# Where the output projection's operand splits stand in the queues, and which engine does the last group's late gating

## The chip, the cores and the metric

The kernel runs on one core of one Trainium2 chip. The metric is the device time of one launch in microseconds (us). A core has engines that work side by side, each through its own queue in order: PE (TensorE, matrix products), ACT (ScalarE), DVE (VectorE), POOL (GpSimd) and SP, which here issues nearly all DMA transfers. An engine whose next instruction waits on a semaphore lets everything behind it in its queue wait too.

## The reference

One decoder layer in float32 over 2048 tokens (16 learned meta tokens go ahead of them), width 1024:

```python
hn = rms_norm(h, norm_g)
proj = einsum('bld,de->ble', hn, w_in)                # 1024 -> 4096
cx, cb, cc, cg, q, k, v, rg = split(proj, 8)          # 512 columns each
conv_out = cb * short_conv(cc * cx, conv_w) * silu(cg)
ret_out  = head_group_norm(retention(rot(q), rot(k), v), ret_norm_g) * silu(rg)
mixed = concatenate([conv_out, ret_out], -1)
h = h + einsum('ble,ed->bld', mixed, w_out)           # 1024 -> 1024
out = rms_norm(h, final_g)[:, N_META:]
```

What matters here is the last product, `mixed` times `w_out`, and the gating `conv_out = (...) * silu(cg)` of the last convolution group, which feeds it.

## The kernel before, in words

**Products.** Each float32 operand is split into a high part (an ACT cast) and a low part (a DVE subtraction), both by `split` (lines 117 to 126), and a product is three matmuls: low by high, high by low, high by high. Blocks of 2 by 2 are multiplied with seven instead of eight block products, so both operands need sums and differences of their blocks. A block product is 12 matmuls of 128x128 by 128x512 (`product` in `quad`, line 275, and in `quads`, line 323).

**Weights and moving operands.** In the output stage the rows of `mixed` are the stationary side ("weights": tiles `wh`, `wl`, in rings of `RING = 3` buffers each, filled by `weight_parts`), and `w_out` is the moving side (tiles `mh`, `ml`, one buffer for each of the seven operands, "slots"). A weight buffer comes free when the product three before it is done.

**Two row halves, then the output.** The loop over `r` runs eight units (heads and convolution groups) for each half of the rows. The last convolution group of a half is called with `last=True`: its products are taken, but its gating is left for later: a function is put in the list `kept`. Then comes the output for eight pairs of row blocks (a pair is 256 rows). Pairs 0 and 1 are done together, turn by turn, by `quads` (turn i does product i of pair 0, then product i of pair 1); pairs 2 to 7 follow one by one in `output`, each with one `quad`.

**The opening of the output.** `moving_in_turn` loads and splits the first block of `w_out` (slot 0), splits the first weights of both pairs ("leading"), then slot 1, and returns steps that are run inside `quads`. `open_output` is run behind turn 0 and traces the splits of three prepared operands: `sums(m, 1)` into slot 2 (tiles `t`), `sums(m, 0)` into slot 3 and `sums(m, 2)` into slot 4 (tiles `held`, loaded long before). Slot i is first used in turn i.

**The late gating.** For each of the last group's two column blocks j: the gate is multiplied by the row factors `rr`, ACT takes Silu of it, the convolution result is multiplied by `rr`, the two are multiplied ("join", on POOL in any case), and the result is stored to `mixed`. In row half 1 the function is called behind pair 2 with POOL for all multiplications. Block j = 0 is in rows that pairs 4 and 5 read, j = 1 in rows that pairs 6 and 7 read. Row half 0's gating is called in `close_sums`, with DVE.

**An output pair.** `stationary` makes four sums of the pair's blocks on POOL (`sa`, `ra`), `rows` adds the products to the residual: for products that need two terms, POOL adds the copied term `tc` to `yo` (line 1129), DVE adds the PSUM bank (line 1135). Product 4 and product 6 of a pair accumulate in the same bank, so product 6 can't start until DVE has added the bank as product 4 left it. Then come squares on ACT, the row factor `rf` on POOL (line 420) and the final scaling on ACT (line 1170) and DVE (line 1177).

**What sets the order.** The order of each queue is written at build time by a planner: it takes instructions in the order in which the code traces them, as they become ready by its own costs, with the timeline simulation that the last lines of `kernel` ask for. `tc.issue_after(ins)` puts everything that a block traces on the engine of `ins` behind `ins` in that engine's queue, and nothing else; instructions on other engines, DMA issues on SP among them, are not held by it. `queued` does so for several instructions. The names that carry instructions for this: `lowered[0]` (the last DVE split), `copied[0]` (the last ACT copy of a bank), `summed[0]` (the last POOL sum of a pair's blocks), `leads[0]` (pair 0's split of this turn), `loaded[0]` and `line[0]` (DMA issues).

Of the kernel before, what the change touches and what calls it, by code (L numbers as in the profile page):

```python
# [12 lines left out]
AF = mybir.ActivationFunctionType  # L13
# [66 lines left out]
def hybrid_trunk(ctx: ExitStack, tc: tile.TileContext, t, out: bass.AP, chunk_decay):  # L80
# [5 lines left out]
    nc = tc.nc  # L86
# [18 lines left out]
    def brief(name="b"):  # L105
        return sb.tile([P, HB + 128], F32, name=name, tag="b", bufs=BRIEF)[:, :HB]

    lowered, third, fifth, given, summed = [None], [None], [None], [None, None], [None]

    @contextmanager  # L110
    def queued(instructions):
        with ExitStack() as order:
            for ins in instructions:
                order.enter_context(tc.issue_after(ins.ins))
            yield

    def split(hi, lo, src, scale=None, eng=nc.vector):

        if scale is None:
            nc.scalar.copy(out=hi, in_=src)  # L120
            lowered[0] = eng.tensor_tensor(out=lo, in0=src, in1=hi.bitcast(F32), op=ALU.subtract)  # L121
            return
        scaled[0] = nc.scalar.mul(hi, src, scale)
        nc.vector.scalar_tensor_tensor(
            out=lo, in0=src, scalar=scale, in1=hi.bitcast(F32), op0=ALU.mult, op1=ALU.subtract
        )
# [71 lines left out]
    def moving_in_turn(load, scale, sums, ws):  # L198


        m = [[] for _ in range(8)]

        def blocks(half, j, kts=range(KH)):
            for kt in kts:
                k = half * KH + kt
                parts(m, BLOCK[half][j], kt, load(k, j), scale(k) if scale else None)

        blocks(0, 0)
        leading = [next(a) for a in ws]
        blocks(1, 0, range(KH // 2))  # L210
        with tc.issue_after(copied[0].ins):
            blocks(1, 0, range(KH // 2, KH))
        steps = [
            lambda: sums(m, 1), lambda: sums(m, 0), lambda: sums(m, 2), lambda: blocks(1, 1), lambda: sums(m, 3),
        ]
        return m, leading, steps
# [93 lines left out]
    def quads(ws, w, m, takes, between=()):  # L310


        between = iter(between)
        banks = [[None, None] for _ in ws]
        copies = [None for _ in ws]

        def product(n, i, bank, first):
            wh, wl = w[n]
            for kt in range(KH):
                ks = slice(kt * P, (kt + 1) * P)  # L320
                mh, ml = m[i][kt]
                for s, (a, b) in enumerate(((wl, mh), (wh, ml), (wh, mh))):
                    nc.tensor.matmul(  # L323
                        bank, a[:, ks], b, start=first and kt == 0 and s == 0, stop=kt == KH - 1 and s == 2,
                        skip_group_check=not first,
                    )

        def copy(bank):
            c = sb.tile([P, HB], F32, name="tc", tag="tc", bufs=COPIES)
            copied[0] = nc.scalar.copy(out=c, in_=bank)  # L330
            return c

        for i in range(7):
            for n in range(len(ws)):
                if i < 2:
                    banks[n][i] = ps_proj()
                product(n, i, banks[n][i in (1, 3, 5)], i in (0, 1, 3))
            w = [next(a, None) for a in ws[:1]]
            leads[0] = lowered[0]
            w += [next(a, None) for a in ws[1:]]  # L340
            for n, take in enumerate(takes):
                bank = banks[n][i in (1, 3, 5)]
                if i == 0:
                    copies[n] = copy(bank)
                elif i == 1:
                    take(0, 0, bank, copies[n])
                elif i == 2:
                    copies[n] = [copy(bank)]
                elif i == 3:
                    copies[n].append(copy(bank))  # L350
                elif i == 4:
                    take(1, 1, bank, copies[n][1])
                elif i == 5:
                    take(0, 1, bank, copies[n][0])
                else:
                    take(1, 0, bank, None)
            next(between, idle)()
# [285 lines left out]
    def store_mixed(r, j, kt, m):  # L643
        d = mixed[2 * r + j]
        nc.sync.dma_start(
            d[:, :, kt // KH, :, kt % KH, :].rearrange("a i p c -> p a i c"),
            m.rearrange("p (a i c) -> p a i c", a=2, i=2),
        )
# [77 lines left out]
    kept = []  # L726

    def conv_group(g, r, m, f, blocks, ahead, steps=(), last=False):


        def go_on():
            next(factors_ahead[0], None)

        def behind(quad, *own):
            return [lambda n=n: (own[n](), go_on() if (quad, n) in steps else None) for n in range(3)]

        u = [gen("u") for _ in range(2)]
        rr, rr2 = ([a[:, j * HB : (j + 1) * HB] for j in range(2)] for a in f[:2])
        held = [None]
        behind_head = r == 0 and len(waiting[1]) + len(waiting[0]) > 0  # L740

        def mul(eng, out, a, b):
            eng.tensor_tensor(out=out, in0=a, in1=b, op=ALU.mult)  # L743

        def take(i, j, pp, c):
            s = u[j][:, 2:]
            if c is None:
                mul(nc.vector, s, pp, s)
            elif i == 1:
                add(nc.vector, c, pp, c)  # L750
                held[0] = c
            else:
                add(nc.vector, s, pp, c)
                with queued((fifth[0],) if behind_head and j == 0 else ()):
                    mul(nc.vector, s, s, rr2[j])
                if j == 1:
                    mul(nc.gpsimd, s, s, held[0])

        blocks, meta = blocks
        quad(stationary(blocks, keep=kept_sums(2 * (NG + g), r)), m, take, behind(0, lambda: finish_late(behind_head and not waiting[0]), idle, idle))  # L760
        catch_up(0)
        if meta:
            meta_carry(g, meta)
        carry(u, g, r)
        cs = [taps(u[j], g) for j in range(2)]
        gates = []

        ungated = []

        def gated():  # L770
            if last:
                return
            j, c = gates.pop()
            nc.scalar.activation(c, c, AF.Silu)
            mul(nc.gpsimd, cs[j], cs[j], rr[j])
            mul(nc.gpsimd, cs[j], cs[j], c)

        def take(i, j, pp, c):
            if i == 0:
                if last:  # L780
                    gate = brief("cg")
                    add(nc.vector, gate, pp, c)
                    ungated.append(gate)
                    return
                add(nc.vector, c, pp, c)
                mul(nc.vector, c, c, rr[j])
                gates.append((j, c))
                if j == 1:
                    gated()
                return  # L790
            if c is not None:
                add(nc.vector, c, pp, c)
                pp = c
            taken[0] = nc.vector.tensor_tensor(out=cs[j], in0=pp, in1=cs[j], op=ALU.mult)

        n = 2 * (NG + g) + 1
        quad(stationary(load_raw(w_loads(n, r)), keep=kept_sums(n, r)), m, take, behind(1, idle, gated, idle))
        blocks = ahead()
        def store():
            for j in range(2):  # L800
                store_mixed(r, j, g, cs[j])

        def gate_late(eng):
            for j, gate in enumerate(ungated):
                mul(eng, gate, gate, rr[j])
                nc.scalar.activation(gate, gate, AF.Silu)
                mul(eng, cs[j], cs[j], rr[j])
                mul(nc.gpsimd, cs[j], cs[j], gate)
            return store

        if last:
            kept.append(gate_late)
        else:
            store()
        return blocks
# [416 lines left out]
    for r in range(NR):  # L1232
# [82 lines left out]
        else:  # L1315
# [10 lines left out]

            def close_sums(t4=first[4]):
                t4()
                with tc.issue_after(lowered[0].ins):
                    store_kept = kept.pop()(nc.vector)  # L1330
                with tc.issue_after(loaded[0].ins):
                    store_kept()

            first = [(ws, leading), open_sums, first[3], close_sums]
            between = (), idle, idle, idle
# [44 lines left out]
                a[0](i, j, in_line)  # L1380

    def open_output():
        for a in first[:3]:
            a()
        fetch((0, 0))

    def fourth():
# [11 lines left out]
    quads(ws, leading, m, [a[1] for a in two], (open_output, idle, fourth, fifth_pair))  # L1399
    for a in two:  # L1400
        a[3]()
    for pair in range(2, SEQ // (2 * P)):
        output(pair, m, final_g)
        if pair == 2:
            with tc.issue_after(summed[0].ins):
                kept.pop()(nc.gpsimd)()


# [36 lines left out]
```

## Time and profile before

| | |
|---|---|
| median of 3 runs | 864.91 us (864.87 to 866.22) |
| profiled execution | 866.39 us, of which span 864.60 us |
| instructions | 12843 |
| PE busy | 850.8 us (98%) |
| DVE busy | 688.9 us (80%) |
| ACT busy | 498.7 us (58%) |
| POOL busy | 286.7 us (33%) |
| mean granted PE clock | 0.994 |

The span is what lies between the first and the last instruction; the execution's own time has some more around it. A row of the timeline gives the start and the duration in us, engine, line, operation, output<-inputs, and in brackets the idle time before it with what ended it. Matmul rows overlap: each is shown with about 0.39 us, while they start every 0.227 us at full clock. A row of the stretches gives for each engine the busy time and the number of instructions, then the granted PE clock as a share of full speed. Output pair 0 and 1 lie between 698.9 and 738.7 us, pair 2 begins at 738.7 us.

### The profile page before, as it was taken

The numbers are of one execution on the slowest core, as the hardware profiler recorded it, in microseconds if no ns is written. First come the engines' busy times: TensorE is split into PE (matmuls) and PEld (weight loads), VectorE is DVE, ScalarE is ACT, GpSimd is POOL, SyncE is SP. The second block draws the span as 40 slices with busy tenths as digits, with TensorE's granted clock in tenths as the row PEclk, the third lists the DMA queues.
The fourth block names the chain that finished last, engine by engine and source line by source line (L and its number), as shares of the span: only waits on it lengthen the run. The fifth ranks groups of instructions, "written<-read, shape, count | busy, mean of one in ns | idle before, by whom it ended". The sixth has DMA issues, their size and how long they took to land.

```text
span 864.6 us, 12843 instructions
## 1 busy us (share of the span) xinstructions
PE 850.8 (98%) x4192; PEld 703.0 (81%) x4192; DVE 688.9 (80%) x1209; ACT 498.7 (58%) x903; POOL 286.7 (33%) x230
## 2 busy tenths in 40 slices
PE   9999999999999999999999999999999989999996
PEld 6778888878887878888888888888888878778885
DVE  6798989889887977999688788877665777876774
ACT  7875648474845655965673848444333656545453
POOL 0022332323245554000001003240523013987873
PEclk9999999999999999999999999999999999999999
DMA  9736357565777743966565756558646666356432
GB/s 323 243 124 170 94 145 217 145 185 183 183 242 233 254 148 110 364 220 159 116 166 161 207 148 167 171 147 287 181 140 183 240 207 223 124 193 191 151 130 78
DMA packets 143779, 158.88 MB, mean 184 GB/s; under 512 B 60192, under 2 KB 78176, under 8 KB 143712
## 3 DMA queue, kind: packets, MB, share of 16 engines
q1 hardware_dynamic: 143136, 157.67, 59.7%
q8 instruction: 33, 0.54, 0.3%
q10 hardware_dynamic: 576, 0.40, 0.1%
q14 instruction: 34, 0.28, 0.1%
HBM read 103.50 MB, written 41.94 MB: 168 GB/s over the span
## 4 chain that ended last, share of the span: by engine, by line
PE 95%; DVE 1%; issue 1%; POOL 1%; ACT 0%; DMA 0%; ACTq 0%; POOLq 0%; DVEq 0%
PE pj L275 72%; PE pj L323 9%; PE pj L405 5%; PE ms L1030 2%; PE ms L1019 2%; PE ms L1029 2%; PE ms L1006 2%; PE ms L579 1%; DVE ml L121 1%; DMA ra<-in_w_in 0%; DVE wl L121 0%; POOL cg L743 0%; PE ms L453 0%; POOL yo L129 0%; PE ms L609 0%
## 5 line engine op out<-in xcount | busy, mean ns | idle before, releaser
L275 PE MATMUL pj<-mh,wl 128*128 128x512 f32 x952 | 374.2, 393 | 2.4 <-DVE wl L121 2.4
L275 PE MATMUL pj<-mh,wh 128*128 128x512 f32 x952 | 372.1, 391 | 0.0
L275 PE MATMUL pj<-ml,wh 128*128 128x512 f32 x952 | 371.5, 390 | 0.0
L120 ACT CAST wh<-ra 128x512 fp32r<-128x512 f32 x244 | 151.1, 620 | 247.9 <-PE pj L275 175.0
L121 DVE TENSOR_TENSOR wl<-ra,wh 128x512 fp32r<-128x512 f32 x244 | 206.9, 850 | 59.9 <-ACT wh L120 58.7
L275 PEld LDWEIGHTS pj<-mh,wl 128*128 128x128 f32 x952 | 179.2, 188 | 40.5 <-DVE wl L121 2.9
L275 PEld LDWEIGHTS pj<-mh,wh 128*128 128x128 f32 x952 | 179.1, 188 | 37.2
L275 PEld LDWEIGHTS pj<-ml,wh 128*128 128x128 f32 x952 | 179.2, 188 | 36.4
L132 POOL TENSOR_TENSOR ra<-ra 128x512 f32<-128x512 f32 x42 | 64.9, 1544 | 78.1 <-PE ms L579 38.6
L1042 POOL TENSOR_TENSOR rp<-rs,neg_half 128x4 f32<-128x4 f32 x16 | 18.4, 1150 | 140.2 <-DVE rs L129 140.1
L282 ACT COPY tc<-pj 128x512 f32<-128x512 f32 x102 | 59.1, 580 | 0.1
L129 POOL TENSOR_TENSOR sa<-ra 128x512 f32<-128x512 f32 x21 | 31.0, 1477 | 55.7 <-DMA ra<-in_w_in 36.3
L323 PE MATMUL pj<-mh,wl 128*128 128x512 f32 x112 | 44.5, 397 | 2.6 <-DVE wl L121 2.6
L323 PE MATMUL pj<-mh,wh 128*128 128x512 f32 x112 | 44.2, 395 | 0.0
L323 PE MATMUL pj<-ml,wh 128*128 128x512 f32 x112 | 44.1, 394 | 0.0
L1146 POOL TENSOR_TENSOR z<-yo,final_g 128x512 f32<-128x512 f32 x16 | 26.3, 1646 | 51.2 <-DVE yo L1135 49.7
L132 POOL TENSOR_TENSOR ra<-sa,ra 128x512 f32<-128x512 f32 x21 | 30.0, 1430 | 31.2 <-DVE wl L121 23.0
L1135 DVE TENSOR_TENSOR yo<-pj,yo 128x512 f32<-128x512 f32 (+1 forms) x33 | 22.1, 672 | 17.4 <-POOL yo L129 8.4
L1046 DVE TENSOR_SCALAR pm<-ms,mv,rp 128x128 f32<-128x128 f32 x64 | 21.9, 405 | 9.1 <-POOL rp L1042 9.1
L1177 DVE SCALAR_TENSOR_TENSOR yo<-yo,rf,final_g 128x512 f32<-128x512 f32 (+1 forms) x17 | 20.1, 1193 | 10.2 <-POOL rf L420 9.4
L323 PEld LDWEIGHTS pj<-mh,wl 128*128 128x128 f32 x112 | 21.4, 191 | 7.6 <-DVE wl L121 3.2
L129 POOL TENSOR_TENSOR yo<-yo,tc 128x512 f32<-128x512 f32 x18 | 26.4, 1474 | 2.7 <-ACT tc L282 2.4
(171 smaller groups left out, 1235.4 us busy)
## 6 DMA issues: line engine op xcount, KB each, us to landing
ra<-in_w_in SPq DMA_DIRECT2D x110, 256.0 KB, 3.0
ra<-sums_a SPq DMA_DIRECT2D x56, 256.0 KB, 3.1
x<-in_xT SPq DMA_DIRECT2D x44, 256.0 KB, 4.9
sums_a<-ra SPq DMA_DIRECT2D x42, 256.0 KB, 2.1
yo<-in_x SPq DMA_DIRECT2D x32, 256.0 KB, 4.7
ra<-mixed SPq DMA_DIRECT2D x30, 256.0 KB, 3.0
w<-in_w_out SPq DMA_DIRECT2D x28, 256.0 KB, 4.7
ra<-in_x SPq DMA_DIRECT2D x16, 256.0 KB, 3.4
```

The costliest lines, as they stand in the source:

```text
L120: nc.scalar.copy(out=hi, in_=src)
L121: lowered[0] = eng.tensor_tensor(out=lo, in0=src, in1=hi.bitcast(F32), op=ALU.subtract)
L129: eng.tensor_tensor(out=out, in0=a, in1=b, op=ALU.add)
L132: return eng.tensor_tensor(out=out, in0=a, in1=b, op=ALU.subtract)
L275: nc.tensor.matmul(bank, a[:, ks], b, start=first and kt == 0 and n == 0, stop=kt == KH - 1 and n == 2, skip_group_check=not first,)
L282: copied[0] = nc.scalar.copy(out=c, in_=bank)
L323: nc.tensor.matmul(bank, a[:, ks], b, start=first and kt == 0 and s == 0, stop=kt == KH - 1 and s == 2, skip_group_check=not first,)
L405: nc.tensor.matmul(banks[n][i], a[:, ks], b, start=half + kt + s == 0, stop=half == 1 and kt == KH - 1 and s == 2,)
L1046: nc.vector.tensor_scalar(out=y[:, cs], in0=o[:, cs], scalar1=mv[:, c, 0:1], scalar2=rp[:, c, :], op0=ALU.subtract, op1=ALU.mult,)
L1135: last[0] = nc.vector.tensor_tensor(out=y[:, cs], in0=pp[:, cs], in1=y[:, cs], op=ALU.add)
L1146: nc.gpsimd.tensor_tensor(out=ys[i][j], in0=y, in1=final_g[:, j * HB : (j + 1) * HB], op=ALU.mult)
L1177: nc.vector.scalar_tensor_tensor(out=here, in0=here, scalar=rs, in1=final_g[:, cs], op0=ALU.mult, op1=ALU.mult)
```

## The change

Two parts, both in the output stage.

First, `split` also keeps its ACT cast in `raised[0]`. `moving_in_turn` keeps the pair (DVE split, ACT cast) of the last leading weights, which are pair 1's, in `head_parts`; `quads` keeps that of pair 0's weights of the next turn in `lead_parts`. `open_output` then traces the splits of slot 2 behind the first, and those of slots 3 and 4 behind the second. The instructions are the same; only places in the ACT and DVE queues are bound.

Second, the late gating is cut into `gate_rows` (two multiplications and Silu), `gate_join` (one multiplication) and `gate_store`. For row half 1, block j = 0 stays on POOL behind pair 2; block j = 1 gets its rows on DVE behind the last weight split of pair 3, its join on DVE behind that of pair 4, and its store there. For row half 0, `close_sums` does what it did, in the same order.

```diff
     def split(hi, lo, src, scale=None, eng=nc.vector):
         if scale is None:
-            nc.scalar.copy(out=hi, in_=src)
+            raised[0] = nc.scalar.copy(out=hi, in_=src)
...
         leading = [next(a) for a in ws]
+        head_parts[0] = lowered[0], raised[0]
...
             leads[0] = lowered[0]
+            lead_parts[0] = lowered[0], raised[0]
...
-        def gate_late(eng):
-            for j, gate in enumerate(ungated):
-                mul(eng, gate, gate, rr[j])
-                nc.scalar.activation(gate, gate, AF.Silu)
-                mul(eng, cs[j], cs[j], rr[j])
-                mul(nc.gpsimd, cs[j], cs[j], gate)
-            return store
+        def gate_rows(j, eng):
+            mul(eng, ungated[j], ungated[j], rr[j])
+            nc.scalar.activation(ungated[j], ungated[j], AF.Silu)
+            mul(eng, cs[j], cs[j], rr[j])
+
+        def gate_join(j, eng):
+            mul(eng, cs[j], cs[j], ungated[j])
+
+        def gate_store(j):
+            store_mixed(r, j, g, cs[j])
...
     def open_output():
-        for a in first[:3]:
-            a()
+        for a, parts_ahead in zip(first[:3], (head_parts, lead_parts, lead_parts)):
+            with queued(parts_ahead[0]):
+                a()
         fetch((0, 0))
...
+    gate_rows, gate_join, gate_store = kept.pop()
     for pair in range(2, SEQ // (2 * P)):
         output(pair, m, final_g)
         if pair == 2:
             with tc.issue_after(summed[0].ins):
-                kept.pop()(nc.gpsimd)()
+                gate_rows(0, nc.gpsimd)
+                gate_join(0, nc.gpsimd)
+                gate_store(0)
+        elif pair == 3:
+            with tc.issue_after(lowered[0].ins):
+                gate_rows(1, nc.vector)
+        elif pair == 4:
+            with tc.issue_after(lowered[0].ins):
+                gate_join(1, nc.vector)
+                gate_store(1)
```

More of the change, by code (lines that the diff above doesn't have):

```diff
@@ L106, in brief @@
         return sb.tile([P, HB + 128], F32, name=name, tag="b", bufs=BRIEF)[:, :HB]
-    lowered, third, fifth, given, summed = [None], [None], [None], [None, None], [None]
+    lowered, raised, third, fifth, given, summed = [None], [None], [None], [None], [None, None], [None]
+    head_parts, lead_parts = [()], [()]
     @contextmanager
@@ L801, in store @@
                 store_mixed(r, j, g, cs[j])
-        def gate_late(eng):
-            for j, gate in enumerate(ungated):
-                mul(eng, gate, gate, rr[j])
-                nc.scalar.activation(gate, gate, AF.Silu)
-                mul(eng, cs[j], cs[j], rr[j])
-                mul(nc.gpsimd, cs[j], cs[j], gate)
-            return store
+        def gate_rows(j, eng):
[6 more added lines that the diff above has]
+            store_mixed(r, j, g, cs[j])
         if last:
-            kept.append(gate_late)
+            kept.append((gate_rows, gate_join, gate_store))
         else:
@@ L1328, in close_sums @@
                 t4()
+                gate_rows, gate_join, gate_store = kept.pop()
                 with tc.issue_after(lowered[0].ins):
-                    store_kept = kept.pop()(nc.vector)
+                    for j in range(2):
+                        gate_rows(j, nc.vector)
+                        gate_join(j, nc.gpsimd)
                 with tc.issue_after(loaded[0].ins):
-                    store_kept()
+                    for j in range(2):
+                        gate_store(j)
             first = [(ws, leading), open_sums, first[3], close_sums]
@@ L1401, in hybrid_trunk @@
         a[3]()
+    gate_rows, gate_join, gate_store = kept.pop()
     for pair in range(2, SEQ // (2 * P)):
```

## The prediction

> **What bounds the kernel now.** I read the page first (engine shares, chain), then the list of PE's waits, then PE's timeline at each wait, and last the queues of the engines that those waits name.
>
> ```profile
> PE 850.8 (98%) x4192; PEld 703.0 (81%) x4192; DVE 688.9 (80%) x1209; ACT 498.7 (58%) x903; POOL 286.7 (33%) x230
> PE 95%; DVE 1%; issue 1%; POOL 1%; ACT 0%; DMA 0%; ACTq 0%; POOLq 0%; DVEq 0%
> ```
> ```profile
> PE pj L323 <- DVE wl L121: 2.6, 1, 2.6
> PE pj L275 <- DVE wl L121: 2.4, 1, 2.4
> ```
>
> PE is the bound: 98% busy, 95% of the chain. A change of DVE, ACT or POOL work pays only where PE waits. PE waits long in two places, once each, both for the low part of a weight: at the start of the turns (line 323) and in an output pair (line 275). Both lie where the diff works.
>
> ```profile
> 695.97 0.39 PE L275 MATMUL pj<-mh,wh 128*128 128x512 f32 x1
> 698.91 0.50 PE L323 MATMUL pj<-mh,wl 128*128 128x512 f32 x1 [2.56 <-DVE wl L121]
> 704.06 0.39 PE L323 MATMUL pj<-mh,wl 128*128 128x512 f32 x1
> 738.74 0.39 PE L275 MATMUL pj<-mh,wl 128*128 128x512 f32 x1
> 754.83 0.39 PE L275 MATMUL pj<-mh,wh 128*128 128x512 f32 x1
> 757.66 0.50 PE L275 MATMUL pj<-mh,wl 128*128 128x512 f32 x1 [2.44 <-DVE wl L121]
> 761.87 0.40 PE L275 MATMUL pj<-mh,wh 128*128 128x512 f32 x1
> ```
> ```profile
> 698.90:704.05 5.15, 5.14 (x15) 4.06 (x16) 3.02 (x6) 0.71 (x2) 0.00 (x0) 0.67 0.52 159
> 757.65:761.86 4.21, 4.20 (x11) 3.31 (x12) 2.34 (x3) 0.60 (x2) 4.21 (x4) 0.59 0.99 300
> 690.00:696.20 6.20, 6.20 (x29) 4.92 (x27) 6.20 (x11) 6.20 (x13) 0.00 (x0) 1.00 1.05 395
> 781.20:800.30 19.10, 19.10 (x86) 15.71 (x85) 12.16 (x18) 9.68 (x20) 13.91 (x12) 1.00 0.55 178
> ```
>
> Between 704.06 and 738.74 lie 153 of the 168 matmuls of the turns, so one takes 34.68/153 = 0.2267 us and a product of 12 takes 2.72. The first stretch rows show more than a wait: behind each gap the granted clock is 0.67 and 0.59, against 1.00 elsewhere. First place: the next matmul was due at 696.20, and full speed is back at 704.06 with 15 matmuls done, worth 3.40: 7.86 - 3.40 = **4.46 us** lost (2.71 gap, 1.75 slow clock). Second place: due at 755.06, back at 761.87 with 11 matmuls, worth 2.49: 6.81 - 2.49 = **4.32 us** (2.60 gap, 1.72 clock). Together 8.78 us, the most that can come back.
>
> **First part: the casts at the opening.**
>
> ```profile
> 678.95 0.95 SPq L535 DMA_DIRECT2D ra<-mixed  x2
> 687.73 1.66 ACT L120 CAST mh<-held 128x512 fp32r<-128x512 f32 x3
> 689.29 0.62 ACT L120 CAST wh<-ra 128x512 fp32r<-128x512 f32 x1
> 694.98 0.62 ACT L120 CAST wh<-ra 128x512 fp32r<-128x512 f32 x1
> 696.54 1.14 ACT L120 CAST wh<-ra 128x512 fp32r<-128x512 f32 x2
> 698.17 0.69 DVE L121 TENSOR_TENSOR wl<-ra,wh 128x512 fp32r<-128x512 f32 x1
> L121 DVE TENSOR_TENSOR ml<-held,mh x8: 684/686/690, 688.5 to 698.8; 128x512 fp32r<-128x512 f32 x8
> L121 DVE TENSOR_TENSOR ml<-t,mh x4: 684/688/691, 694.6 to 700.0; 128x512 fp32r<-128x512 f32 x4
> ```
>
> The cast at 689.29 is the last group's seventh weight; that at 694.98 is pair 0's first, whose low part (698.17) releases PE. Its ring buffer was free when the group's fifth product ended, 696.20 - 2 x 2.72 = 690.76, and its block had been asked for at 678.95. What kept it back is the queue: between 690 and 696.20 ACT and DVE are busy without a break, in good part with `held` and `t`, the operands of slots 2 to 4. The edit changes no instruction and no DMA issue (SP isn't bound by it); it puts four `t` splits behind pair 1's first weights and eight `held` splits behind pair 0's second. Then pair 0's cast goes at about 690.8, its low part at 691.5 to 692.2, due at 696.20: some 4 us early. The 2.71 and the 1.75 go.
>
> What is late next? Pair 1's first weights: buffer free at 693.48, low part done by about 694.8, due 698.92. Pair 0's second: free at 696.20, done 697.6, due 701.64. Then the eight `held` splits: in a row DVE starts one each 0.60, 4.8 in all, until 702.4. If all stand ahead of pair 1's second weights these are done at 703.1, due 704.36. Slot 2 is used first at 696.20 + 4 x 2.72 = 707.1, slot 3 at 712.5. ACT has the same twelve casts at 0.52. Every margin is positive, the smallest 1.2, so I take 0 as cost, with 1 us as the upper bound; gain **4.46**.
>
> **Second part: the gating.**
>
> ```profile
> L743 POOL TENSOR_TENSOR cg<-cg,rr x2: 1284/1286/1287, 739.6 to 742.6; 128x512 f32<-128x512 f32 x2
> L743 POOL TENSOR_TENSOR c<-c,rr x2: 1741/1750/1759, 740.9 to 743.8; 128x512 f32<-128x512 f32 x2
> L743 POOL TENSOR_TENSOR c<-c,cg x2: 1466/1598/1730, 747.0 to 751.9; 128x512 f32<-128x512 f32 x2
> 753.57 0.54 POOL L420 TENSOR_TENSOR rf<-rs_v,neg_half 128x1 f32<-128x1 f32 x1
> 758.71 1.73 POOL L129 TENSOR_TENSOR yo<-yo,tc 128x512 f32<-128x512 f32 x1
> 741.66 0.62 ACT L120 CAST wh<-sa 128x512 fp32r<-128x512 f32 x1
> 754.14 0.72 ACT L1170 ACTIVATE z<-z,rf 128x512 f32<-128x512 f32 x1 [2.03 <-POOL rf L420]
> 754.77 1.15 ACT L120 CAST wh<-ra 128x512 fp32r<-128x512 f32 x2
> 754.14 1.79 DVE L1177 SCALAR_TENSOR_TENSOR yo<-yo,rf,final_g 128x512 f32<-128x512 f32 x1 [1.69 <-POOL rf L420]
> 755.86 1.75 DVE L121 TENSOR_TENSOR wl<-ra,wh 128x512 fp32r<-128x512 f32 x1
> 760.47 0.69 DVE L1135 TENSOR_TENSOR yo<-pj,yo 128x512 f32<-128x512 f32 x1 [1.17 <-POOL yo L129]
> ```
>
> POOL is full through pair 2: in an ordinary pair it has 13.91 of 19.10 us (the stretch from 781.2), the six gate multiplications add 2 x (1.29 + 1.75 + 1.60) = 9.3, so 23.2 us of work for 19.1. So the row factor at 753.57 is late; the ACT scaling and the DVE scaling at 754.14 wait for it, and behind them stand the cast at 754.77 and its low part at 755.86, which PE waits for. Counting from the `sa` cast (weight 3, 741.66), three more belong to pair 2, so that at 754.77 is pair 3's first weight: the planner has put pair 3's product 0 ahead of pair 2's product 6.
>
> The edit takes three of the six away: 4.6 us. POOL then has 18.5 us for 19.1. The row factor comes at about 749.0, so ACT and DVE are free when the ring buffer is (pair 2's product 4 ends at 752.34): cast 752.4, low part done by 753.7 to 754.8, due 755.06. The gap goes, with its 1.72 of slow clock: **4.32**. Against that stands the bank that product 6 needs: DVE reads it at 760.47, behind the POOL addition at 758.71. Both 4.6 earlier: read by 756.6. If the planner, seeing less POOL work, puts product 6 back at 755.06, PE waits 1.5; if it keeps pair 3's product ahead, nothing. Bounds 0 and 1.5; I take **0.7**, the middle, having no row for the new order.
>
> The moved work goes to DVE:
>
> ```profile
> 792.88 1.30 DVE L121 TENSOR_TENSOR wl<-ra,wh 128x512 fp32r<-128x512 f32 x1 [1.67 <-ACT wh L120]
> 796.62 0.69 DVE L1135 TENSOR_TENSOR yo<-pj,yo 128x512 f32<-128x512 f32 x1 [2.43 <-POOL yo L129]
> 793.60 2.98 POOL L129 TENSOR_TENSOR yo<-yo,tc 128x512 f32<-128x512 f32 x2
> 749.50 4.50 SPq L645 DMA_DIRECT2D mixed<-c  x2
> 809.47 3.72 SPq L1185 DMA_DIRECT2D ra<-mixed  x3
> 757.66 99.87 PE pj L275 x432
> ```
>
> Pair 4 shows the place: behind a pair's last weight split (792.88) DVE idles 2.43 us until POOL has added, then reads the bank, until 797.31. From 757.66 PE runs 432 matmuls without a break, so pair 4's product 6 is due at 761.87 + 157 x 0.2267 = 797.46: 0.15 us of slack. In pair 3 two multiplications go into such a hole, each 0.69 (the read at 796.62) to 1.75 (the split at 755.86, with POOL busy): 1.4 to 3.5 for 2.43, so 0 to 1.1 over; the two POOL additions (2.98) may stretch to 2 x 1.73, 0.5 more. Bounds 0 and 1.5; I take 0.3, nearer the short end, because DVE's part fits unless every row is a slow one. In pair 4 one multiplication fits: 0. The Silu sits on ACT, idle for half of such a pair (9.68 of 19.10). The second store leaves the place where SP stands 4.50 us at 749.50 and comes in pair 4, at about 797; its readers are asked for from 809.47. Cost 0; were the store 10 us late, those loads would be.
>
> The Trainium skill, GPSIMD Engine Reference, section Specifications, says that GpSimd's SBUF interfaces are shared with VectorE and contend with DVE instructions that have two SBUF inputs; by that rule the moved multiplications still slow POOL, and pair 3 pays its upper 1.5. The trace agrees on the contention (splits of 0.69 and of 1.75), and the result would be 858.3.
>
> **Sum.** 4.46 + 4.32 - 0.7 - 0.3 = 7.8 us. The profiled span of 864.60 becomes 856.8. That execution took 866.39, 1.48 above the median of the runs; I take the gain off the median: 864.91 - 7.8 = **857.1 us**.
>
> **Rivals.**
> *Second part pays half.* POOL stays late enough that product 6 waits 1.5 or more and the clock falls again: the trace shows falls only behind 2.4 us and more, so for 1.5 between 0 and 1.72. Gain 4.46 + 0 to 1.1 - 0.3: 859.6 to 860.8. For it: 0.15 us of slack; against: POOL's 18.5 of 19.1. 0.16.
> *First part fails.* The planner sets other work, as the four `t` casts, so that PE waits as long: gain 4.32 - 1.0, 861.6. 0.06.
> *The slow clock isn't the gaps'.* Then 1.75 and 1.72 stay: 864.91 - 5.31 + 1.0 = 860.6. Against: the stretches at 1.00 on both sides. 0.04. The Trainium skill, TensorE: Matmul & The Clock Gate, section "HAM oscillation — how this bites in real kernels", gives as its abstract rule that idle gaps above about 3.4 us make the clock fall; by that rule these gaps wouldn't, and this rival would hold. The trace differs: gaps of 2.71 and 2.60 are each followed by 0.67 and 0.59.
> *No change.* Both waits move elsewhere for the same price: 864.9. 0.05.
> *Slower.* New bounds make the planner set one more POOL operation (1.73) ahead of the additions in pairs 3 to 7. With 0.15 of slack each pair then waits 1.6, and if the clock falls each time 1.72 more: 5 x 3.3 = 16.5, so 864.9 - 8.8 + 16.5 = 872.6. It decides from 8.78/5 = 1.76 per pair. Against: those pairs run without a break and nothing in them is edited beyond pair 4. 0.06.
>
> **How the numbers follow.** The forecast has 0.63. The range 855.9 (all 8.78 back, and a little scatter) to 860.8 holds it, the half and the clock: 0.83. Alone, the likeliest case has 856.1 to 859.4 (remainders 0 to 3). About 0.2%, 1.7 us, can be told from no change; faster holds all cases but the last two: 0.89, 0.05, 0.06.
>
> **What would show it.** In the new profile the wait of line 323 is gone, no `held` cast stands ahead of pair 0's first weights, and the stretch behind has clock 1.00. In pair 2 POOL has three gate multiplications, and PE no wait above 1.5. Two gate multiplications of DVE follow pair 3's last weight split, one pair 4's. A PE wait for `yo` of line 1135 in pairs 2 to 4 is the remainder that I priced at 1.0; several of them, or a clock below 1.00 behind them, make the prediction wrong.

## The result, and the profile after

The changed kernel takes 860.33 us (median of 4 runs, 859.72 to 860.47) against 865.57 us for the kernel before on the same chip (4 runs, 864.87 to 867.12): ratio 0.9936, 95% interval 0.9918 to 0.9953. That is 5.2 us less; the forecast was 7.8 less, at 857.1, with 855.9 to 860.8 as range. The interval leaves out 1, so the gain is clear of the noise. The time lies inside the range, near its upper end, and above 856.1 to 859.4, which the prediction gave for its likeliest case alone. The profiled execution took 859.72 us with a span of 857.9 (before: 866.39 and 864.6).

The lines below have moved: 121 is now 122, 275 is 277, 323 is 325, 1135 is 1141 (and in kernels further below 1141 moves on to 1144 in `fewer` and 1149 in `thin_a` and `thin_b`). First the list of PE's waits (us in total, times, longest) and PE's rows at the opening, then DVE's there:

```profile
PE pj L277 <- DVE yo L1141: 1.3, 3, 0.5
PE pj L277 <- DVE wl L122: 0.3, 1, 0.3
```
```profile
695.67 0.39 PE L277 MATMUL pj<-mh,wh 128*128 128x512 f32 x1
695.90 0.39 PE L325 MATMUL pj<-mh,wl 128*128 128x512 f32 x1
```
```profile
697.65 0.68 DVE L122 TENSOR_TENSOR wl<-ra,wh 128x512 fp32r<-128x512 f32 x1
698.25 4.90 DVE L122 TENSOR_TENSOR ml<-held,mh 128x512 fp32r<-128x512 f32 x8
703.07 0.68 DVE L122 TENSOR_TENSOR wl<-ra,wh 128x512 fp32r<-128x512 f32 x1
```

Both long waits are gone. PE goes over into the turns without a break (0.23 us from 695.67 to 695.90). The eight `held` splits now stand behind pair 0's second weight, and pair 1's second ends at 703.75, where the forecast had 703.1; its product is due at 695.90 + 36 x 0.2267 = 704.06. What is left are four small waits. The stretches show where they are: from 695.90 the opening, then pairs 2, 3, 4 and 5 (columns PE, PEld, DVE, ACT, POOL, granted clock, DMA share, GB/s):

```profile
695.90:701.05 5.15, 5.15 (x24) 4.29 (x23) 5.15 (x10) 5.14 (x11) 0.00 (x0) 1.00 1.05 397
733.98:754.39 20.41, 19.57 (x85) 15.61 (x84) 17.71 (x17) 11.02 (x22) 19.61 (x15) 1.00 0.54 178
754.39:773.96 19.57, 19.34 (x85) 15.69 (x84) 16.78 (x20) 10.20 (x21) 15.14 (x12) 1.00 0.59 188
773.96:793.80 19.84, 19.33 (x85) 15.70 (x84) 14.79 (x19) 9.68 (x20) 14.70 (x12) 1.00 0.37 117
793.80:812.84 19.04, 19.04 (x85) 15.77 (x84) 13.91 (x18) 9.72 (x20) 15.04 (x12) 1.00 0.67 224
```

The clock is 1.00 in each. A pair of 84 matmuls takes 84 x 0.2267 = 19.04 us, as pair 5 does; pair 2 is 1.37 over it, pair 3 0.53, pair 4 0.80: **2.70 us**, forecast as 0.7, 0.3 and 0. PE's rows at the four waits, two in pair 2, one each in pairs 3 and 4:

```profile
748.06 0.47 PE L277 MATMUL pj<-mh,wl 128*128 128x512 f32 x1 [0.32 <-DVE wl L122]
751.54 0.50 PE L277 MATMUL pj<-mh,wl 128*128 128x512 f32 x1 [0.51 <-DVE yo L1141]
771.11 0.50 PE L277 MATMUL pj<-mh,wl 128*128 128x512 f32 x1 [0.23 <-DVE yo L1141]
790.95 0.50 PE L277 MATMUL pj<-mh,wl 128*128 128x512 f32 x1 [0.51 <-DVE yo L1141]
```

The brackets hold only the time in which PE is shown idle. By the starts of the matmuls the waits are 0.48, 0.67, 0.39 and 0.67 us, and the matmul behind each starts some 0.1 late too: 2.6 of the 2.70. The first is for the low part of a weight (product 5 of pair 2), the others are for the bank that product 6 needs.

From profile to profile: the first place gives back 2.71 of gap and 1.75 of clock (the turns, from their first matmul to pair 2, take 38.08 instead of 39.83), the second 4.32 - 2.70 = 1.62 (pairs 2 to 7: 118.39 before, 116.71 now, with 0.06 from the other pairs). The start of the turns is 0.30 earlier for other reasons and the end behind the last matmul 0.26 shorter: 864.6 - 857.9 = 6.7.

### The profile page after: what moved, and what is told of

It is laid out like the page before. It is cut to its first block, busy times and chain, and to the rows that moved or that the text cites. A ratio compares the mean times of both kernels' runs of the same rounds, so it can differ in the third digit from the quotient of the medians.

```text
span 857.9 us, 12855 instructions
## 1 busy us (share of the span) xinstructions
PE 848.2 (99%) x4192; PEld 700.7 (82%) x4192; DVE 692.4 (81%) x1212; ACT 499.5 (58%) x903; POOL 282.2 (33%) x227
## 4 chain that ended last, share of the span: by engine, by line
PE 93%; POOL 2%; issue 1%; DVE 1%; DMA 1%; ACT 0%; ACTq 0%; POOLq 0%; DVEq 0%; SPq 0%
PE pj L277 71%; PE pj L325 9%; PE pj L408 5%; PE ms L1036 2%; PE ms L1025 2%; PE ms L1035 2%; PE ms L1012 2%; PE ms L582 1%; POOL yo L130 1%; POOL ra L133 1%; DMA ra<-in_w_in 0%; DVE yo L1141 0%; DVE wl L122 0%; DMA yo<-in_x 0%; DVE yo L1183 0%
## 5 line engine op out<-in xcount | busy, mean ns | idle before, releaser
L277 PEld LDWEIGHTS pj<-mh,wl 128*128 128x128 f32 x952 | 178.8, 188 | 40.6 <-DVE yo L1141 2.5
L663 DVE SCALAR_TENSOR_TENSOR c<-u,conv_w,c 128x512 f32<-128x512 f32 x32 | 25.2, 831 | 2.3 <-POOL u L654 1.2
```

The lines of the kernel that those rows point to most:

```text
L277: nc.tensor.matmul(bank, a[:, ks], b, start=first and kt == 0 and n == 0, stop=kt == KH - 1 and n == 2, skip_group_check=not first,)
L663: nc.vector.scalar_tensor_tensor(out=c, in0=u[:, tap : tap + HB], scalar=conv_w[:, g, tap : tap + 1], in1=c, op0=ALU.mult, op1=ALU.add)
```

## The experiments

The main theory: two separate losses, each returned by its own part of the change, and the small waits are the price of the gating operations at their new places. Each run is compared with the kernel before on the same chip.

**One part alone.** `p1_only` keeps the first part and does the gating as before, all six operations on POOL in pair 2; `p2_only` is the other way round.

```diff
# p1_only
         if pair == 2:
             with tc.issue_after(summed[0].ins):
-                gate_rows(0, nc.gpsimd)
...
+                for j in range(2):
+                    gate_rows(j, nc.gpsimd)
+                    gate_join(j, nc.gpsimd)
...
# p2_only
-        for a, parts_ahead in zip(first[:3], (head_parts, lead_parts, lead_parts)):
-            with queued(parts_ahead[0]):
-                a()
+        for a in first[:3]:
+            a()
```

> The first part of the change alone: the operand splits of the output's opening stand behind the weights, all late gating stays on GpSimd in pair 2 as before. Theory (the two parts act on two separate losses): the gap at the start of the turns and the slow clock behind it are gone (4.46 us), the 2.4 us wait in pair 2 and its slow clock stay as they were (4.32 us); span about 860.2, time 4.5 us under the kernel before. Rival (the two waits are linked, the second is the echo of the first): with the first gap gone the wait in pair 2 shrinks too, span 858 or less.

> The second part alone: the gating is divided over pairs 2 (GpSimd), 3 and 4 (VectorE), the opening is as before. Theory: the gap of 2.6 us at the start of the turns and its slow clock stay; in pairs 2 to 4 the 4.32 us are gone and 2.7 us of small waits come in their place, as in the changed kernel: gain 1.6 us, span about 863.0. Rival: the small waits come from the first part's shift of work, so that this half alone gains nearly the whole 4.3 us: span 860.3.

`p1_only`: 862.14 us (861.73 to 862.29), ratio 0.9963 [0.9949, 0.9977], span 860.1. `p2_only`: 863.20 us (862.54 to 864.98), 0.9978 [0.9968, 0.9987], span 863.0. PE's rows at the waits that stay, first of `p1_only`, then of `p2_only`:

```profile
753.25 0.50 PE L277 MATMUL pj<-mh,wl 128*128 128x512 f32 x1 [2.45 <-DVE wl L122]
```
```profile
699.26 0.50 PE L325 MATMUL pj<-mh,wl 128*128 128x512 f32 x1 [2.63 <-DVE wl L122]
```

Each part removes its own wait and leaves the other; in `p2_only` the small waits are there with the same sizes (0.49, 0.67, 0.38 and 0.65 by the starts of the matmuls). The two losses are separate, and the savings of 0.37% and 0.22% come to 0.59%, against 0.64% for both together, well inside the intervals. The runs of `p2_only` fall into two groups: seven with a mean granted clock of 0.998 or 0.999 took 862.5 to 863.8 us, four with 0.996 or 0.997 took 864.7 to 865.0. The profiled one is of the second group and shows a fall of the clock behind its gap.

**The whole gating in the turns.** `turn_gate` keeps the first part; all six operations go to POOL in the turns, behind its first two scalings by the final gain (`z`), where POOL sits idle for 12 us.

```diff
+    def gate_in_turns():
+        with tc.issue_after(gained[0].ins):      # gained[0]: the last z on POOL
+            for j in range(2):
+                gate_rows(j, nc.gpsimd)
+                gate_join(j, nc.gpsimd)
+                gate_store(j)
...
-    quads(..., (open_output, idle, fourth, fifth_pair))
+    quads(..., (open_output, gate_in_turns, fourth, fifth_pair))
```

> The changed kernel with its first part as it is, and the last group's whole gating (both blocks) on GpSimd inside the turns of pairs 0 and 1, queued behind the multiplications by final_g of the first two outputs, where GpSimd is idle for some 12 us. Theory (the waits of 2.7 us in pairs 2 to 4 are the price of the gating there): no wait of PE above 0.1 us is left in pairs 2 to 4, span 855.2, time 2.7 us under the changed kernel. Rival 1 (an ordinary pair has so little slack at the bank that product 6 needs that pairs 2 to 4 wait anyway): 0.4 to 0.7 us in each stay, span 857. Rival 2 (GpSimd's work in the turns slows VectorE's weight splits): a new wait in the turns, span 858 or more.

861.26 us (861.12 to 862.44), ratio 0.9958 [0.9945, 0.997], span 860.6. Pairs 2 to 7 take 19.04 us each: without gating in them there is no wait, so the 2.70 are its price. But the turns pay. The first two rows are DVE's row for the same four splits in the changed kernel and here, the third POOL's beside it here, the last PE's wait:

```profile
711.36 2.50 DVE L122 TENSOR_TENSOR ml<-w,mh 128x512 fp32r<-128x512 f32 x4 [0.31 <-ACT mh L121]
```
```profile
712.61 6.91 DVE L122 TENSOR_TENSOR ml<-w,mh 128x512 fp32r<-128x512 f32 x4
717.21 3.43 POOL L746 TENSOR_TENSOR c<-c,cg 128x512 f32<-128x512 f32 x2
```
```profile
PE pj L325 <- DVE wl L122: 2.4, 1, 2.4
```

Four splits take 2.50 us alone and 6.91 beside POOL's multiplications. PE's wait is for a weight's low part that stands behind them in DVE's queue, and the clock falls behind it (0.60 from 721.24 to 725.50). The turns take 42.43 us instead of 38.08: they lose 4.35 where the pairs save 2.70.

**The gap filled.** `fill_gap` is the kernel before with 11 matmuls of a constant tile in the gap at the opening, to see whether the slow clock behind it is the gap's.

```diff
+    with tc.issue_after(multiplied[0].ins):      # the last matmul ahead of the output
+        warm_up(11)
     quads(...)
```

> The kernel before with 11 more matmuls of zeros (128x128 by 128x512, into a bank that nothing reads) put between the last product of the row halves and the first of the turns, where PE stands for 2.6 us; nothing else is changed. Theory (the slow clock behind the gap comes from the gap): PE still waits for the same weight, but is busy meanwhile; the granted clock stays at 1.00 behind it and the 1.75 us come back, span 862.9. Rival (the clock falls there for another reason, a time or a kind of instruction): the clock falls to 0.67 all the same, span 864.6 or, where the matmuls delay the product, more.

864.86 us (864.21 to 865.78), ratio 0.9992 [0.9982, 1.0001]. There was no slow clock behind the filled gap. But there was none behind the unfilled one in pair 2 either, which was 2.61 us long; its stretch in this run:

```profile
757.30:761.50 4.20, 4.20 (x18) 1.00 0.96 301
```

Where the kernel before had 11 matmuls in such a stretch at a clock of 0.59, this run had 18 at 1.00. So this run can't say what the filling did; it says that a gap alone doesn't decide.

**The second block not gated; fewer operations at each place.** Both kernels start from the changed one and leave multiplications out.

```diff
# j0only: no gate_rows(1, ...) in pair 3, no gate_join(1, ...) in pair 4
# fewer: pair 2 without gate_join(0, ...), pair 3 one multiplication, pair 4 none
```

> The changed kernel without the gating of the second block: the two VectorE row multiplications in pair 3 with the Silu between them and the VectorE join in pair 4 are left out; the second block is stored as it is. Theory (each pair's small waits are the price of that pair's own gating operations, because GpSimd and VectorE slow each other): pair 2 keeps its 1.37 us, pairs 3 and 4 go back to 19.04 us each, so the span is 857.9 - 0.53 - 0.80 = 856.6. Rival (a pair that came late leaves the next one late, so pair 4's wait is pair 3's or pair 2's): pair 3 or 4 keeps a wait of 0.4 to 0.7 and the span is 857.1 to 857.4.

> The changed kernel with fewer of the gating operations at each place: pair 2 has GpSimd's two row multiplications but not the join, pair 3 one VectorE multiplication in place of two (that of the block, not that of its gate, which gets no Silu), pair 4 none; the output lacks these products. Theory (each pair has about 1 us of room between the bank's last read and the product that needs the bank, as the pairs without gating show, so the last operation at each place makes the wait): pair 2 costs 0 to 0.4 us instead of 1.37, pair 3 0 to 0.1 instead of 0.53, pair 4 nothing; span 857.9 - 1.2 - 0.5 - 0.8 = 855.4. Rival (the price goes with the number of operations): pair 2 costs 0.9, pair 3 0.27, span 856.4.

`j0only` took 858.69 us (one run, span 856.9), `fewer` 858.55 (one run, 856.8). Pair times from PE's rows, in us; the last two lines are told of further below:

| kernel | pair 2 | pair 3 | pair 4 |
|---|---|---|---|
| changed | 20.41 | 19.57 | 19.84 |
| `j0only` | 20.46 | 19.04 | 19.07 |
| `fewer` | 19.27 | 19.04 | 19.36 |
| `turn_gate` | 19.04 | 19.04 | 19.04 |
| `thin_b` | 19.04 | 19.04 | 19.04 |

In `j0only` pair 2 keeps its price and pairs 3 and 4 lose theirs: no wait is handed on from pair to pair. In `fewer` the third operation of pair 2 carries 1.1 of its 1.4 us, and one multiplication in pair 3 is free: in these single runs the price is not in proportion to the number, a place has room up to a point. The miss is pair 4, which has no gating and still waits 0.32. Its rows, of DVE's read of the bank:

```profile
789.00 0.69 DVE L1144 TENSOR_TENSOR yo<-pj,yo 128x512 f32<-128x512 f32 x1 [2.44 <-POOL yo L130]
```

Product 6 was due six products behind the pair's start, 773.24 + 6 x 2.72 = 789.56; the read ended at 789.69. In `turn_gate` it ended 0.76 ahead of its due time (792.96 for 793.72). So pair 4's own room changes from kernel to kernel by nearly 1 us and can be nothing. The span of 856.8 also holds 0.95 us from ahead of pair 2, which starts at 734.93 here and at 733.98 in the changed kernel. Two profiles of one kernel differ there too, by 0.25 (the changed kernel, 734.23 in `after_again`) and by 0.46 (`thin_b`, 734.84 and 734.38); why it is 0.95 here isn't shown.

**The gating thinned out.** `thin_a` and `thin_b` do all of it, on POOL. In `thin_a` the first block's three operations stand in the turns; in `thin_b` two do, and its join is the one extra operation at pair 2's head. In both the second block's three stand one in each of pairs 2, 3 and 4, behind the pair's last POOL addition. (The code binds them behind the addition traced before the last; in the traces they stand behind both, in `thin_b` at 749.25, 768.42 and 788.15.)

```diff
+    def gate_in_turns():
+        with tc.issue_after(gained[0].ins):
+            gate_rows(0, nc.gpsimd)              # thin_a: gate_join(0), gate_store(0) too
...
         if pair == 2:
             with tc.issue_after(summed[0].ins):  # thin_b only
                 gate_join(0, nc.gpsimd)
                 gate_store(0)
+            with tc.issue_after(earlier[0].ins): # the POOL addition traced before the pair's last
+                gate_gate(1, nc.gpsimd)
+        elif pair == 3: ... gate_row(1, nc.gpsimd)
+        elif pair == 4: ... gate_join(1, nc.gpsimd); gate_store(1)
```

> All of the gating, thinner: the first block's three operations on GpSimd in the turns behind the first two scaled rows (where GpSimd sits idle for 12 us), the second block's three on GpSimd too, one in each of pairs 2, 3 and 4 behind the pair's last GpSimd addition. Theory (a price arises only where more operations stand together than the place has room for; the six together in the turns delayed VectorE's splits by 5.7 us and made a wait of 2.6, so there is room for about 3): the turns cost 0 to 0.3, pairs 2 to 4 are 19.04 us each, span 855.2 to 855.5, and the time is 2.5 us below the changed kernel's, about 857.7. Rival 1 (room in the turns is less than three operations need): a wait of 0.5 to 1.5 there, perhaps with a slow clock behind it, span 856 to 858. Rival 2 (an operation behind the last addition delays the next pair's first raw sums): 0.4 to 0.7 in each of pairs 3 to 5, span 856.5 to 857.3.

> As the thinner gating with three operations in the turns, but only the first block's two row multiplications stand there and its join is GpSimd's single extra operation at the head of pair 2; the second block's three operations stand one each behind the last GpSimd addition of pairs 2, 3 and 4. Theory: no place has more than its room; span 855.2 to 855.4, time about 857.6. Rival 1 (one operation at pair 2's head already costs): 0.4 to 0.7 there, span 855.7 to 856.0. Rival 2 (the one behind the last addition delays the next pair): span 856.5 to 857.3, as in the other.

`thin_b`: 857.53 us (857.14 to 857.91), ratio 0.9903 [0.989, 0.9916], no wait in the output. `thin_a`: 861.92 us (860.68 to 863.02), 0.9953 [0.994, 0.9966], span 860.0: its pairs are clean too, but PE waits once in the turns, with a slow clock behind it. The rows: PE's wait, then ACT's in `thin_a`, then ACT's in `thin_b`:

```profile
725.99 0.50 PE L325 MATMUL pj<-mh,wl 128*128 128x512 f32 x1 [1.79 <-DVE wl L122]
```
```profile
719.28 0.62 ACT L121 CAST mh<-t 128x512 fp32r<-128x512 f32 x1
723.98 0.63 ACT L1156 ACTIVATE rot<-yo 128x512 f32<-128x512 f32 x1 [4.08 <-DVE yo L1149]
724.52 0.19 ACT L1156 ACTIVATION_READ_ACCUMULATOR rot<-yo 128x1 f32 x1
724.61 1.12 ACT L121 CAST wh<-ra 128x512 fp32r<-128x512 f32 x2
```
```profile
719.21 0.62 ACT L121 CAST mh<-t 128x512 fp32r<-128x512 f32 x1
719.73 0.62 ACT L121 CAST wh<-ra 128x512 fp32r<-128x512 f32 x1
722.80 0.63 ACT L1156 ACTIVATE rot<-yo 128x512 f32<-128x512 f32 x1 [2.46 <-DVE yo L1149]
```

In `thin_b` ACT casts the next weight at 719.73 and then waits for a bank to be read; in `thin_a` the planner put the same cast behind that wait, and it comes at 724.61. It is neither theory nor rival: with the join in the turns another order came out in ACT's queue. DVE was slower there as well, by 1.1 us in the four splits that were shown for `turn_gate` (first `thin_a`, then `thin_b`):

```profile
712.56 4.70 DVE L122 TENSOR_TENSOR ml<-w,mh 128x512 fp32r<-128x512 f32 x4
```
```profile
712.49 3.60 DVE L122 TENSOR_TENSOR ml<-w,mh 128x512 fp32r<-128x512 f32 x4
```

So these splits took 2.50, 3.60, 4.70 and 6.91 us with none, two, three and six POOL multiplications placed there. What the 1.1 us alone would have cost PE, with ACT's queue as in `thin_b`, isn't shown.

**Once more on one chip.** `thin_b`, the changed kernel and the kernel before, all unaltered.

> The thinner gating (the first block's two row multiplications in the turns, its join alone at pair 2's head, the second block's three operations one behind the last GpSimd addition of pairs 2, 3 and 4) once more, on the same chip as the changed kernel. Theory: pairs 2 to 7 take 19.04 us each again, the span is 855.2 to 856.2 and the time 2.5 to 3 us below the changed kernel's. Rival (its first time was a better chip, not a better order): less than 1 us below the changed kernel's.

> The changed kernel unaltered, beside the thinner one. Theory: the four small waits stay (2.70 us in pairs 2 to 4), no slow clock in the output's part, time 860.0 to 860.6. Rival: the small waits are a matter of the run as the slow clock is, and the sum over pairs 2 to 4 comes out below 2 or above 3.4.

> The kernel before unaltered, for its profile. Theory (the two gaps of 2.71 and 2.60 us are in every run, the 1.7 us of slow clock behind each is not): the gaps are there within 0.1 us, and the profiled execution's time is 863.0 to 863.5 plus 1.7 for each gap that has a slow clock behind it. Rival (the slow clock follows each gap every time, and the spread of the runs comes from elsewhere): both gaps have their 7 to 8 half-speed steps whatever the time is.

`thin_b_again`: 857.46 us (857.41 to 857.88), ratio 0.9902 [0.9887, 0.9917]. `after_again`: 860.26 us (859.93 to 862.78, where the highest isn't explained), 0.9938 [0.9924, 0.9953], small waits of 0.49, 0.65, 0.39 and 0.59, pairs 2 to 4 together 2.64 over three undisturbed pairs (57.12). The thinner version is 2.8 us below the changed kernel, 0.33%.

`before_again` is the surprise: 865.93 us in the median, and a profiled execution of 865.38 (span 863.6) that has both gaps and no slow clock. PE's waits, and the stretches behind the first gap, behind the second, pair 2 and pair 3 (PE, clock, DMA share, GB/s):

```profile
PE pj L323 <- DVE wl L121: 2.6, 1, 2.6
PE pj L275 <- DVE wl L121: 2.4, 1, 2.4
PE pj L275 <- ACT tc L282: 1.6, 2, 0.8
```
```profile
699.70:703.90 4.20, 4.18 (x18) 1.00 0.41 121
756.80:760.90 4.10, 4.02 (x17) 1.00 0.94 302
737.97:759.77 21.80, 19.38 (x85) 1.00 0.50 162
759.77:779.93 20.16, 19.34 (x85) 1.00 0.56 189
```

The gaps are fixed, as expected, and the slow clock is a matter of the run. But the price expected for it was wrong: without either, 863.0 to 863.5 was due and 865.38 came. The same pairs in the first profile of the kernel before, where the clock fell:

```profile
738.74:762.10 23.36, 20.93 (x85) 0.93 0.54 174
762.10:781.15 19.05, 19.05 (x86) 1.00 0.53 169
```

With the slow clock the two pairs take 42.41 us, without it 41.96: pair 2 is 1.56 shorter, and pair 3 1.11 longer, since PE now waits there for one of ACT's copies (`tc`; 0.82 us idle at 774.36). Two more profiles have this gap in pair 2: `p1_only`, where the clock fell, takes 42.44 for the two pairs, `fill_gap`, where it didn't, 41.97. So in these four the second slow stretch costs 0.45 at the end, not 1.72; the first costs 1.58 (the turns: 39.83 with it, 38.25 without). The spans are 1.0 apart: 1.58 and 0.45 less, 0.81 more because the turns start later in this run (699.72 for 698.91), 0.22 more in pair 4. The 0.81 is for the most part another wait for an ACT copy, long before the output (0.76 us idle at 275.97), which the first profile doesn't have.

## Why the prediction was right, and where it was off

**Right: the two gaps, their places and their causes.** `p1_only` and `p2_only` show each gap to be a queue's order and each part to remove one. The first part came out as it was worked out: pair 0's cast starts at 690.66 (forecast 690.8), its low part ends at 692.09 (692.2), and PE doesn't wait. Only the smallest margin, 1.2 us for pair 1's second weight, shrank to 0.3 (703.75 for 704.06).

**By its own sign the second part's working failed.** The prediction named several waits of PE for `yo` in pairs 2 to 4 as something that makes it wrong, and three came. The second part gave back 1.62 us of its 4.32, where 4.32 - 1.0 = 3.32 had been worked out. That the time still lies in the range is in part luck. The range was drawn wide enough for two rivals, "second part pays half" (859.6 to 860.8) and "the slow clock isn't the gaps'" (860.6), and 860.33 lies where these two had been priced; but neither happened in the changed kernel, whose clock is 1.00 behind each small wait and whose product 6 waits less than 1.5.

**Off: the three remainders, 2.70 instead of 1.0.** In pair 2 the planner did put product 6 back at its natural place, the case for which 1.5 was named as bound; the middle of 0 and 1.5 was taken where nearly the bound came, 1.37. PE waits twice there: 0.48 for the low part of product 5's weight, for which the working had no term, and then 0.67 for the bank. The bank decides: without any wait product 6 was due at 733.98 + 16.32 = 750.30, and DVE's read ends at 751.49. The read waits for POOL:

```profile
747.33 3.43 POOL L130 TENSOR_TENSOR yo<-yo,tc 128x512 f32<-128x512 f32 x2
```
```profile
750.80 0.69 DVE L1141 TENSOR_TENSOR yo<-pj,yo 128x512 f32<-128x512 f32 x1 [1.19 <-POOL yo L130]
```

The working counted POOL's hours for the pair (18.5 of 19.1) and didn't ask when in the pair they fall; `fewer` shows that the join alone, at the pair's head, carries 1.1. The hours were low too: POOL was busy 19.61 of 20.41. In pair 3 0.53 came for 0.3, inside its bounds: the two multiplications take 1.77 and 1.78 and DVE reads the bank behind them, until 771.05, for a product 6 that was due at 770.71.

```profile
766.97 1.77 DVE L746 TENSOR_TENSOR cg<-cg,rr 128x512 f32<-128x512 f32 x1
768.67 1.78 DVE L746 TENSOR_TENSOR c<-c,rr 128x512 f32<-128x512 f32 x1
770.37 0.68 DVE L1141 TENSOR_TENSOR yo<-pj,yo 128x512 f32<-128x512 f32 x1
```

In pair 4 "one multiplication fits: 0" failed: the 0.15 us of slack had been quoted in the same paragraph, and the hole that the multiplication was to use is one in which DVE waits for POOL, whose additions it lengthens. POOL's two additions and DVE's join and read in the changed kernel:

```profile
786.73 3.44 POOL L130 TENSOR_TENSOR yo<-yo,tc 128x512 f32<-128x512 f32 x2
```
```profile
787.24 1.78 DVE L746 TENSOR_TENSOR c<-c,cg 128x512 f32<-128x512 f32 x1
790.20 0.69 DVE L1141 TENSOR_TENSOR yo<-pj,yo 128x512 f32<-128x512 f32 x1 [1.18 <-POOL yo L130]
```

The join takes 1.78, and the additions 3.44 instead of 2.98; the read ends at 790.89, product 6 was due at 773.96 + 16.32 = 790.28. The same two additions take 3.44 in pair 3 and 3.00 in pair 5 of this kernel, and 2.98 to 3.00 in pairs 3 and 4 of `j0only`, which has no gating there. The stretch of 0.5 that was priced for pair 3 was left out for pair 4; it is most of the 0.6, and the rest is the room of pair 4, which differs from kernel to kernel.

The Trainium skill's rule (GPSIMD Engine Reference, Specifications) that GpSimd contends with VectorE instructions that have two SBUF inputs was given as speaking against pair 3. The trace agrees on the contention in pairs 3 and 4 alike (1.77 and 1.78 for DVE's multiplications, 3.44 for POOL's additions), but not on the price drawn from it for pair 3: 0.53 came, not 1.5.

**Off: what the gain was taken from.** 7.8 was worked out on an execution of 866.39 in which the clock fell twice, and taken off 864.91, a median of three runs. That median was low: with a fourth run it is 865.57, and later sets of the same kernel have medians of 865.85 to 866.38. And an execution without the falls has less to give back: in `before_again` it is 2.75 at the first gap, 0.17 in the turns and 3.88 in pairs 2 and 3, 6.8 in all instead of 8.78. The runs' mean clocks show the two ends of this only: of the kernel before's runs the nine with 0.993 took 866.3 to 867.4, the three with 0.999 864.5 to 865.4, and those between, 0.994 to 0.997, lie anywhere from 864.2 to 867.7. The changed kernel's runs all have 0.998 or 0.999. 1.7 for the remainders and 1.48 for the base are the 3.2 between 857.1 and 860.3; they come out so evenly because two other terms cancel, the 0.56 that the profiled execution gained ahead of the turns and behind the last matmul, and the 0.61 by which the changed kernel's median lies above its profiled execution.

**The rival on the clock** ("the slow clock isn't the gaps'") is half true. It was worth 0.04 because both gaps of the profile were followed by a fall; two profiles here have gaps of 2.58 to 2.75 with none. The Trainium skill's rule (TensorE: Matmul & The Clock Gate, "HAM oscillation — how this bites in real kernels") that idle gaps above about 3.4 us make the clock fall agrees, taken as a threshold, with those profiles. It doesn't agree with the five falls behind gaps of 2.6 to 2.8 (both of the first profile, one each in `p1_only`, `p2_only` and `turn_gate`), nor with a sixth behind 1.95 in `thin_a` (by the starts of the matmuls; 1.79 idle). What decides isn't settled: no run here sets the gap's length or its moment by itself.

## What to carry to other kernels

Price a moved operation by the queue that stands behind it at that place, not by the engine's free time in the whole stage: behind POOL's last addition one extra operation was free in all three pairs tried, while the one beside that addition, ahead of the bank's read, cost pair 4 up to 0.8 us. When a stage has no room, thin the work out: at most two operations at a place, and those with room behind them, gave 2.8 us more than the same six in three places (number and place changed together, so how much each brought isn't shown). And take a gain off the execution from which it was worked out; before you take it off a median, see whether the loss is in every run and whether the median has enough runs.

## What the runs showed of the hardware

- VectorE and GpSimd slow each other here: a DVE subtraction of 128x512 is shown with 0.69 us while POOL is idle and with 1.75 and more beside POOL (four of them took 2.50 and 6.91), a DVE multiplication with 1.77 to 1.78 beside POOL, and two POOL additions in a row with 3.44 in the two pairs of the changed kernel that have a DVE multiplication beside them (3 and 4) and 3.00 in the next two, which have none. So an operation moved from POOL to DVE still slowed POOL.
- A gap of 2.6 to 2.8 us on PE is followed by some 4 us at a granted clock of 0.59 to 0.67 in some executions and by full clock in others of the same kernel. One wait of 1.95 us (`thin_a`) was followed by such a fall too (0.65).
- A slow stretch can cost less than it shows: 1.72 us of slow clock in pair 2 cost 0.45 at the end, by two profiles with it and two without; where the clock stayed up, PE waited for a copy by ACT in pair 3 instead.
